# Bidirectional hybrid encoder layer on one core: when the output weights, the convolution's first tile and the first modulation scales are prepared

## The chip, the cores and the metric

One core of a Trainium2 chip runs the whole layer; the other cores are idle. The metric is the time of one execution in microseconds (us), the median of several runs. Engines are called by the profile's names: PE (TensorE), DVE (VectorE), ACT (ScalarE), POOL (GpSimd) and SP (SyncE, which issues all transfers here). Each works through its own instructions in a fixed order and waits where an input or a buffer is not ready.

## What is computed

One transformer-like layer over 2048 tokens of width 1024, in float32:

```
mod = silu(c) @ w_ada + b_ada            # shift1, scale1, gate1, shift2, scale2, gate2
u   = adaln(x) * (1 + scale1) + shift1
q, k, v, glu = split(u @ w_in)
attn = rms(attention(rope(rms(q)), rope(rms(k)), v))      # 8 query heads, 2 kv heads of 64
h    = rms(swish(LN(depthwise31(a * sigmoid(g)))) @ w_pw2)  # 512 channels
x   = LN(alpha*x + gate1 * (concat(attn, h) @ w_o))
ffn = (gelu(conv3(up_g)) * conv3(up_v)) @ w_down            # width 2816
x   = LN(alpha*x + gate2 * ffn)
```

Matrix products run on values that are split into a high part in a matmul format (`wh`, `uh`) and the rest (`wl`, `ul`); each product is three matmuls (`mm3`, L117 to L119). ACT makes the high part (`split`, L123), DVE or POOL subtracts it to get the low part (L126).

## The kernel before, in words

The program has three stages.

**Projections (0 to 400 us).** Sixteen tiles of 128 tokens are normalised, transposed, modulated and multiplied by `w_in`. The modulation vectors come first: `ada_first(hf)` multiplies `silu(c)` with half of the first two blocks of `w_ada`, eight rows of 128 per block, mostly on DVE (L261, L263, tile `acc`) and partly on PE (L266); PE sums over the partitions (L270) and DVE moves shift and scale into `mc[hf]` (L274). For tiles 0 to 2 the products with the first four rows of `w_in` (`lo`) are made as soon as `mc[0]` is there, while `ada_first(1)` still runs. `half(s, 0)` modulates tile s: ACT and POOL each take two of four blocks `u` (L318, L320), then ACT makes `uh`, DVE `ul`. `load_w("kv", True, lo)` loads and splits the key and value columns; `later` holds the two splits of the query columns, whose low parts go to DVE and POOL in turn.

**Attention (400 to 1260 us).** There are 16 units of two heads and 512 queries; each runs 16 steps over blocks of 128 keys (`unit_main`): four score matmuls (L576, L577), two exponentials on ACT (L578, tile `pr`), and four matmuls with the values (L587). Row sums of `pr` are added up by POOL in 12 steps (`lp`, L605 and L608) and by DVE in four (`ld`); in the last unit DVE takes 12 and POOL four. `unit_end` first adds `lp` and `ld` on DVE (L527). After each step `step()` advances three kinds of generators, whose order of `yield` thus sets the order of work: the ends of older units, the preparation of the next unit (`unit_prep`: eight transposes into PSUM, q splits on ACT and DVE L169, 32 matmuls L177 whose maxima DVE reduces in L179, then L186 and L188, which give the next unit's scores their offset), and, from unit 1 on, `conv`.

`conv_work` is one generator: 16 tiles of four groups of channels (`front`: POOL makes the band matrices `tz`, L676, ACT gathers `hg`; `mid`: PE transposes `hg` and ACT writes `hT`; 12 matmuls L695, L701 on DVE), then four chunks (layer norm on DVE, swish, `w_pw2`, norm), and last `load_wo`: for each of 16 pieces of `w_o` DVE multiplies by the gate (L630, tile `rw`), ACT makes `woh`, DVE subtracts (L126, tile `wol`), with two yields a piece. Its line in `step()`:

```
if state["unit"] > 0:
    drain(conv, 2 if state["n"] % 6 == 0 else 1)
```

There are 240 steps from unit 1 on, and in 40 of them `conv` advances twice: 280 advances. The generator has 254 yields.

**Output projection, channel mixer.** `out_mm` multiplies the concatenated heads with `woh` and `wol`; PE's order puts the first of these matmuls among the last steps of the last unit. Then come layer norms and the channel mixer as a Strassen-like product (1450 to 2839 us).

The engine orders are drawn up by a scheduler from the program's order, priorities and its own estimate of durations; `tc.issue_after(ins)` adds that what is traced in the block comes behind `ins` on `ins`'s engine, and leaves other engines free. PSUM has eight banks of 128x512 (`bank()`), handed out in rotation: a matmul into a bank waits for the last reader of what lay there.

Of the kernel before, what the change touches and what calls it, by code (L numbers as in the profile page):

```python
# [13 lines left out]
ALU = mybir.AluOpType  # L14
# [19 lines left out]
def layer_kernel(ctx, tc, x, cT, w_ada, b_ada, b_adaT, w_in, qg2, kg2, rope, conv_t, cmask, mmask,  # L34
# [100 lines left out]
    kv = ExitStack()  # L135
# [58 lines left out]
    with ExitStack() as ph:  # L194
# [36 lines left out]
        def load_w(n, stage=False, ks=range(KD), engines=(V,), wait=False):  # L231
            c0, w = chunks[n]
            kk = D // w
            jobs = []
            for i, k in enumerate(ks[::kk]):
                raw = t4k((P, kk, w), stage)
                SY.dma_start(raw, w_in[k * P:(k + kk) * P, c0:c0 + w].rearrange("(k p) c -> p k c", p=P))
                jobs.append((wih[n][:, k:k + kk, :], wil[n][:, k:k + kk, :], raw, None, engines[i % len(engines)]))
                if not wait:
                    split(*jobs.pop())  # L240
            return jobs
# [4 lines left out]
        def ada_first(hf):  # L246
# [24 lines left out]
                             rhs=ones[:, 0:1], start=False, stop=True, skip_group_check=True)  # L271
            mc[hf] = wks.tile([P, 2, 4], F32, name="mc%d" % hf)
            for v in range(2):
                V.tensor_scalar(mc[hf][:, v], pm[:, v * 4:v * 4 + 4], float(v), None, op0=ALU.add)  # L274

        def ada_later():

# [23 lines left out]
        def normed(xt):  # L301
            mu, r = ln_stats(wks, xt, "ln0")
            nm = wks.tile([P, 1], F32, name="ln0_n", bufs=3)
            G.tensor_scalar(nm, mu, r, -1.0, op0=ALU.mult, op1=ALU.mult)
            A.activation(xt, xt, AF.Identity, scale=r, bias=nm)
            return xt
# [96 lines left out]
        lo, hi = range(4), range(4, KD)  # L403
        xs = [normed(load_x(0)), normed(load_x(1))]
        drain(ada_first(0))
        load_w("kv", True, lo)
        xs.append(load_x(2))
        later = load_w("q", True, lo, (V, G), True)
        ada = ada_first(1)
        next(ada)  # L410
        us = {s: u_tiles() for s in range(3)}
# [15 lines left out]
        for n in ("kv", "q"):  # L427
            for s in range(3):
                if (s, n) == (2, "kv"):
                    normed(xs[2])  # L430
                    flip(2)
                    half(2, 0)
                pss[s, n] = proj(us[s], n, None, lo)
                drain(ada, None if (s, n) == (0, "q") else 1)
# [214 lines left out]
    def conv_work():  # L649
# [32 lines left out]
            A.activation(hT[:, :, 1:129], pq.rearrange("p (g b) -> p g b", g=4), AF.Copy)  # L682

        f = front(0)
        mid(*f)
        for g4 in range(16):
            hT, hg, tz = f
            if g4 < 15:
                f = front(g4 + 1)
            yield  # L690
            pc = bank()
            for i in range(4):
                tv = tz[:, i].rearrange("p (d s) c -> p d (s c)", d=3)
                for d in range(3):
                    T.matmul(pc[:, i * P:(i + 1) * P], lhsT=hT[:, i, d:d + P], rhs=tv[:, d, :],  # L695
                             start=d == 0, stop=d == 2)
                if i == 1:
                    yield
            for i in range(4):
                g = g4 * 4 + i  # L700
                V.tensor_tensor(hc[:, :, g * 8:(g + 1) * 8],  # L701
                                pc[:, i * P:(i + 1) * P].rearrange("p (s c) -> p s c", c=8),
                                cb[:, g * 8:(g + 1) * 8].unsqueeze(1).broadcast_to([P, NT, 8]), op=ALU.add)
            yield
            if g4 < 15:
                mid(*f)
# [88 lines left out]
    def step():  # L795
        with tc.issue_after(state["s"]):
            for e in list(ends):
                if next(e, "end") == "end":
                    ends.remove(e)
            if preps:  # L800
                drain(preps[0][0], 2 if state["n"] % 2 == 0 else 1)
            if state["unit"] > 0:
                drain(conv, 2 if state["n"] % 6 == 0 else 1)
        state["n"] += 1

    for i, (p, c) in enumerate(units):
# [612 lines left out]
```

## Time and profile before

| what | us |
|---|---|
| three runs, median (lowest to highest) | 2837.76 (2829.4 to 2839.68) |
| the profiled execution, its own time | 2841.01 |
| span of that execution's trace | 2839.1 |
| PE busy | 2682.2 (94%) |
| DVE busy | 2229.9 (79%) |
| ACT busy | 1296.5 (46%) |
| POOL busy | 1252.0 (44%) |

The span runs from the first to the last instruction; about 2 us of the execution lie around it. Busy shares are averages over stages that have different limits, so the place where PE stands still, and what ended that wait, says more than the share.

### The profile page before, as it was taken

To read this page: it belongs to the slowest core of one execution; us is meant where nothing else is said; L and a number is where in the kernel's file an instruction comes from. 1 tells how busy PE (TensorE), PEld (TensorE's weight loads), DVE (VectorE), ACT (ScalarE), POOL (GpSimd) and SP (SyncE) were. 2 spreads that over 40 slices of the span, in tenths; PEclk is the share of its full clock that TensorE was granted. 3 is DMA by queue.
4 is the path that set the end of the run, shared out by engine and by line. 5 is a ranking of instruction groups with operands and counts; after the bars stand their busy time and mean duration, and the time that the engine had idled before them with its cause. 6 is when DMAs were issued, how large, how long until landed. Compare 5 with 4: busy or idle time off the path is not lost.

```text
span 2839.1 us, 35217 instructions
## 1 busy us (share of the span) xinstructions
PE 2682.2 (94%) x12108; PEld 2019.5 (71%) x12108; DVE 2229.9 (79%) x3188; ACT 1296.5 (46%) x2562; POOL 1252.0 (44%) x914
## 2 busy tenths in 40 slices
PE   7999998999999999899988999998999998999996
PEld 6777865766565665467866888886888886876774
DVE  7454465566868768837679989999999888889988
ACT  4333323445545554434454544554554555443442
POOL 3544436886857657533535223324322002335234
PEclk9999999999999999999999999999999999999998
DMA  8343241010101112126766443455444236445542
GB/s 272 95 137 111 80 99 30 25 30 19 30 19 27 30 34 78 41 51 180 232 206 224 134 137 127 143 148 164 139 130 149 81 111 208 148 129 158 163 133 65
DMA packets 336867, 320.59 MB, mean 113 GB/s; under 512 B 70688, under 2 KB 244128, under 8 KB 336688
## 3 DMA queue, kind: packets, MB, share of 16 engines
q1 hardware_dynamic: 336688, 318.34, 37.4%
q8 instruction: 95, 1.56, 0.2%
q14 instruction: 84, 0.69, 0.1%
HBM read 225.71 MB, written 92.55 MB: 112 GB/s over the span
## 4 chain that ended last, share of the span: by engine, by line
PE 67%; DVE 16%; issue 5%; DMA 4%; POOL 4%; ACT 2%; SPq 0%; DVEq 0%; ACTq 0%; POOLq 0%
PE b L1082 32%; PE b L587 6%; PE b L117 5%; PE b L118 5%; PE b L119 5%; PE b L177 4%; PE b L576 3%; PE b L577 3%; DVE wl L126 3%; PE b L131 2%; PE b L695 2%; POOL lp L608 1%; DVE mm L179 1%; DVE o L126 1%; DVE ac L1097 1%
## 5 line engine op out<-in xcount | busy, mean ns | idle before, releaser
L1082 PE MATMUL b<-o,wh 128*128 128x512 f32 x3696 | 1157.7, 398 | 58.2 <-ACT wh L123 22.8
L1082 PEld LDWEIGHTS b<-o,wh 128*128 128x128 f32 x3696 | 698.4, 190 | 232.0 <-ACT wh L123 31.3
L1082 PE MATMUL b<-o,wl 128*128 128x512 f32 x1848 | 717.4, 396 | 8.4 <-DVE wl L126 8.3
L1082 PEld LDWEIGHTS b<-o,wl 128*128 128x128 f32 x1848 | 350.5, 190 | 93.9 <-DVE wl L126 14.5
L608 POOL TENSOR_TENSOR lp<-lp,pr 128x1024 f32<-128x1024 f32 x152 | 382.4, 2516 | 77.0 <-ACT pr L578 69.0
L578 ACT ACTIVATE pr<-b 128x512 f32<-128x512 f32 x512 | 278.4, 597 | 291.1 <-PE b L577 278.7
L179 DVE TENSOR_REDUCE mm<-b 128x1 f32<-128x512 f32 x512 | 321.6, 682 | 113.8 <-PE b L177 112.2
L123 ACT ACTIVATE wh<-wr 128x512 fp32r<-128x512 f32 (+2 forms) x456 | 249.8, 569 | 322.0 <-PE b L1082 201.5
L126 DVE TENSOR_TENSOR wl<-wr,wh 128x512 fp32r<-128x512 f32 (+2 forms) x456 | 334.5, 745 | 14.8 <-ACT wh L123 14.6
L587 PE MATMUL b<-pr,vt 128*64 128x512 f32 x1024 | 244.7, 608 | 4.9 <-ACT pr L578 4.9
L1179 POOL TENSOR_TENSOR cb<-cb,g 128x512 f32<-128x512 f32 x44 | 87.2, 2001 | 326.4 <-DMA cb<-in_w_down_dram 317.7
L576 PE MATMUL b<-q,K 128*128 128x512 f32 x512 | 218.0, 427 | 9.6 <-DVE mm L179 5.5
L577 PE MATMUL b<-q,K 72*128 72x512 f32 x512 | 205.9, 404 | 3.0 <-DVE q L188 3.0
L177 PE MATMUL b<-K,q 128*128 128x512 f32 x512 | 165.8, 421 | 6.1 <-DVE mm L179 5.2
L587 PEld LDWEIGHTS b<-pr,vt 128*64 128x64 f32 x1024 | 66.5, 138 | 131.5 <-issue 113.4
L126 POOL TENSOR_TENSOR o<-stg,o 128x512 fp32r<-128x512 f32 x53 | 81.6, 1540 | 161.6 <-ACT o L123 146.0
L177 PEld LDWEIGHTS b<-K,q 128*128 128x128 f32 x512 | 92.1, 192 | 71.5 <-issue 34.1
L123 ACT ACTIVATE o<-stg 128x512 fp32r<-128x512 f32 x177 | 106.4, 627 | 79.1 <-DMA stg<-w_d 47.7
L576 PEld LDWEIGHTS b<-q,K 128*128 128x128 f32 x512 | 99.2, 194 | 57.4 <-issue 17.8
L1059 POOL TENSOR_TENSOR wr<-wr,wr 128x384 f32<-128x384 f32 (+1 forms) x32 | 34.3, 1073 | 238.1 <-DVE s L1056 227.1
L577 PEld LDWEIGHTS b<-q,K 72*128 72x128 f32 x512 | 99.4, 194 | 20.9 <-issue 3.4
L1097 DVE TENSOR_TENSOR ac<-b,ac 128x512 f32<-128x512 f32 x128 | 87.0, 680 | 24.0 <-PE b L1082 24.0
(259 smaller groups left out, 4922.6 us busy)
## 6 DMA issues: line engine op xcount, KB each, us to landing
wr<-in_w_up_dram SPq DMA_DIRECT2D x88, 512.0 KB
stg<-w_d SPq DMA_DIRECT2D x133, 256.0 KB
g_d<-y SPq DMA_DIRECT2D x44, 512.0 KB
w_d<-cb SPq DMA_DIRECT2D x77, 256.0 KB
wr<-g_d SPq DMA_DIRECT2D x96, 192.0 KB
ar<-in_w_ada_dram SPq DMA_DIRECT2D x64, 256.0 KB
cb<-in_w_down_dram SPq DMA_DIRECT2D x44, 256.0 KB
x<-in_x_dram SPq DMA_DIRECT2D x32, 256.0 KB
```

The lines of the kernel that those rows point to most:

```text
L117: T.matmul(ps, lhsT=wh, rhs=mh, start=first, stop=False)
L118: T.matmul(ps, lhsT=wh, rhs=ml, start=False, stop=False)
L123: A.activation(hi, src, AF.Copy)
L126: (el or V).tensor_tensor(lo, src, hi.bitcast(F32), op=ALU.subtract)
L177: T.matmul(px, lhsT=q1[:, i * P:(i + 1) * P], rhs=K1[:, g, kc * 512:(kc + 1) * 512], start=True, stop=True)
L179: V.tensor_reduce(mm[:, h * 4 + i, kc:kc + 1], px, axis=AX, op=ALU.max)
L576: T.matmul(ps, lhsT=k1, rhs=m1, start=True, stop=False)
L577: state["s"] = T.matmul(ps, lhsT=k2, rhs=m2[0:72], start=False, stop=True).ins
L578: ex = state["exp"] = A.activation(pr[:, i, :], ps, AF.Exp, scale=0.125).ins
L587: state["pv"] = T.matmul(po[i * 64:(i + 1) * 64, :], lhsT=vt[:, kt, g * 64:(g + 1) * 64], rhs=pr[:, i, :], start=kt == 0, stop=kt == NT - ...
L608: eng.tensor_tensor(acc, acc, pr, op=ALU.add)
L1082: T.matmul(ps, lhsT=a[x][:, k, :], rhs=b[y][k], start=first and k == 0 and (x, y) == (0, 0), stop=k == nk - 1 and x == 1, skip_group_check ...
```

## The change

Four edits. (1) `mc["last"]` names the last DVE instruction that writes modulation scales (L274); the splits of the first key and value weights, and later the normalisation of tile 2, are traced behind it, which puts them after it on DVE. (2) The second of the two query splits of `later` goes to DVE, no longer to POOL. (3) Four yields are added at the start of `conv_work`: two between `front(0)` and `mid`, two between `mid` and the loop. (4) `conv` advances twice in every tenth step, no longer in every sixth: 24 of the 240 steps, 264 advances in all, against 258 yields.

```diff
@@ ada_first
-                V.tensor_scalar(mc[hf][:, v], pm[:, v * 4:v * 4 + 4], float(v), None, op0=ALU.add)
+                mc["last"] = V.tensor_scalar(mc[hf][:, v], pm[:, v * 4:v * 4 + 4], float(v), None, op0=ALU.add).ins
@@ first tiles
         drain(ada_first(0))
-        load_w("kv", True, lo)
+        with tc.issue_after(mc["last"]):
+            load_w("kv", True, lo)
         xs.append(load_x(2))
-        later = load_w("q", True, lo, (V, G), True)
+        later = load_w("q", True, lo, (V,), True)
...
                 if (s, n) == (2, "kv"):
-                    normed(xs[2])
+                    with tc.issue_after(mc["last"]):
+                        normed(xs[2])
@@ conv_work
         f = front(0)
+        yield
+        yield
         mid(*f)
+        yield
+        yield
@@ step
-                drain(conv, 2 if state["n"] % 6 == 0 else 1)
+                drain(conv, 2 if state["n"] % 10 == 0 else 1)
```

DVE and ACT near 25 us, where the first scales are ready (`mc` is the scale tile, `wl_kv` and `wl_q` low parts of weights, `ln_st` statistics of tile 2, `u`, `uh`, `ul` the modulated tile). DVE before:

```order
L263 SCALAR_TENSOR_TENSOR acc<-ada,cs,acc 128x512 x6
L126 TENSOR_TENSOR wl_kv<-stage,wh_kv 128x1024
L98 BN_STATS ln_st<-x 128x6 x2
L274 TENSOR_SCALAR mc_197<-b 128x4 x2
L100 BN_AGGR ln_mv<-ln_st 128x2
```

DVE now:

```order
L263 SCALAR_TENSOR_TENSOR acc<-ada,cs,acc 128x512 x6
L274 TENSOR_SCALAR mc_197<-b 128x4 x2
L126 TENSOR_TENSOR wl_kv<-stage,wh_kv 128x1024
L98 BN_STATS ln_st<-x 128x6 x2
L126 TENSOR_TENSOR wl_q<-stage,wh_q 128x1024
```

ACT before, from the first split on:

```order
L123 ACTIVATE wh_kv<-stage 128x1024
L123 ACTIVATE wh_q<-stage 128x1024
L318 ACTIVATE u<-x,mc_197 128x128 x2
L123 ACTIVATE wh_q<-stage 128x1024
L123 ACTIVATE uh<-u 128x512
```

ACT now:

```order
L123 ACTIVATE wh_kv<-stage 128x1024
L318 ACTIVATE u<-x,mc_197 128x128 x2
L123 ACTIVATE wh_q<-stage 128x1024
L123 ACTIVATE uh<-u 128x512
L123 ACTIVATE wh_q<-stage 128x1024
```

The scales moved ahead of one split and the statistics, and the first `uh` ahead of the second query split. On POOL, where a query split stood between the blocks `u` of tiles 0 and 1, four `u` now stand in a row.

PE at the border of units 0 and 1, near 447 us, from the transposes of unit 2's queries on (`hg`, `tz`, `hT` belong to the convolution's first tile). Before:

```order
L131 MATMUL b<-ident,qd 128x128 x8
L131 MATMUL b<-ident,hg 128x128 x4
L576 MATMUL b<-q_3752,K_93 128x512
L577 MATMUL b<-q_3753,K_3723 128x512
L576 MATMUL b<-q_3761,K_93 128x512
L577 MATMUL b<-q_3762,K_3723 128x512
L177 MATMUL b<-K_93,q_4081 128x512 x2
L695 MATMUL b<-tz,hT 128x128 x6
```

Now, from the two L177 on (ahead of them stand the same `qd` and score rows):

```order
L177 MATMUL b<-K_93,q_4081 128x512 x2
L578 MATMUL b<-q_3752,K_93 128x512
L579 MATMUL b<-q_3753,K_3723 128x512
L578 MATMUL b<-q_3761,K_93 128x512
L579 MATMUL b<-q_3762,K_3723 128x512
L177 MATMUL b<-K_93,q_4081 128x512 x2
L589 MATMUL b<-pr,vt 64x512 x2
```

The tile's matmuls left this place for one some 30 PE instructions further on, and the next scores stand in their place. DVE's order at this border is as before: `lp<-lp,ld` (L527), then the two L169, then the maxima.

DVE in the last unit, from its first `ld` on. Before:

```order
L605 TENSOR_TENSOR ld<-pr 128x1024
L608 TENSOR_TENSOR ld<-ld,pr 128x1024
L538 TENSOR_TENSOR osq<-osq,l_10565 128x512
L608 TENSOR_TENSOR ld<-ld,pr 128x1024 x4
L522 SCALAR_TENSOR_TENSOR o<-o,agc,b 128x512
L608 TENSOR_TENSOR ld<-ld,pr 128x1024 x5
```

Now:

```order
L607 TENSOR_TENSOR ld<-pr 128x1024
L126 TENSOR_TENSOR wol_10515<-rw,woh_10514 128x512
L610 TENSOR_TENSOR ld<-ld,pr 128x1024
L540 TENSOR_TENSOR osq<-osq,l_10532 128x512
L126 TENSOR_TENSOR wol_10515<-rw,woh_10514 128x512
L632 TENSOR_TENSOR rw<-rw,row_g_10010 128x512
L610 TENSOR_TENSOR ld<-ld,pr 128x1024
L126 TENSOR_TENSOR wol_10586<-rw,woh_10585 128x512
L632 TENSOR_TENSOR rw<-rw,row_g_10010 128x512
L610 TENSOR_TENSOR ld<-ld,pr 128x1024
L126 TENSOR_TENSOR wol_10586<-rw,woh_10585 128x512
L610 TENSOR_TENSOR ld<-ld,pr 128x1024 x2
```

The last six of the 32 `rw` and `wol` instructions moved behind the last unit's first `ld`. Between the first `ld` of units 12 and 13 there were 11 of them, between those of units 13 and 14 the other 21; now none lies in the first stretch, 11 in the second, 15 between the first `ld` of unit 14 and of unit 15.

## Rows read from the trace of the kernel before

**Rows 1.** The page, part 1: busy time, share of the span, instructions.

```profile
PE 2682.2 (94%) x12108; PEld 2019.5 (71%) x12108; DVE 2229.9 (79%) x3188; ACT 1296.5 (46%) x2562; POOL 1252.0 (44%) x914
```

**Rows 2.** Stretches: PE, PEld, DVE, ACT, POOL busy (instructions); PEclk, DMA share, GB/s.

```profile
440.00:460.00 20.00, 12.29 (x57) 8.44 (x56) 7.14 (x9) 6.95 (x15) 13.57 (x6) 0.83 0.12 26
...
620.00:640.00 20.00, 16.13 (x75) 9.19 (x74) 16.23 (x22) 10.29 (x21) 16.11 (x12) 1.00 0.21 60
...
880.00:900.00 20.00, 16.85 (x73) 10.36 (x73) 18.55 (x16) 13.38 (x27) 15.51 (x8) 0.91 0.15 40
...
1120.00:1140.00 20.00, 14.03 (x42) 8.34 (x43) 20.00 (x18) 6.73 (x13) 16.22 (x7) 0.72 0.20 62
1140.00:1160.00 20.00, 17.38 (x67) 9.96 (x67) 19.94 (x24) 7.38 (x14) 12.08 (x5) 0.86 0.19 62
1160.00:1180.00 20.00, 14.41 (x51) 6.48 (x51) 16.24 (x24) 11.81 (x22) 0.53 (x1) 0.83 0.18 58
```

**Rows 3.** The chain of waits, 1100 to 1200 us: shares by line.

```profile
by line: DVE mm L179 19.9%; DVE rw L630 18.3%; PE b L587 13.2%; DVE wol L126 12.9%; PE b L177 7.9%; PE b L576 4.3%; PE b L577 4.0%; POOL lp L608 3.2%; issue 2.7%; DMA rw<-in_w_o_dram 2.6%; DVE ld L605 2.1%; ACT pr L578 1.7%; DVE osq L538 1.
```

**Rows 4.** Tiles rw, wol and lp: duration ns min/median/max, first to last start.

```profile
L630 DVE TENSOR_TENSOR rw<-rw,row_g x16: 673/684/2866, 1102.7 to 1177.5; 128x512 f32<-128x512 f32 x16
L126 DVE TENSOR_TENSOR wol<-rw,woh x16: 671/692/2286, 1106.4 to 1179.6; 128x512 fp32r<-128x512 f32 x16
L608 POOL TENSOR_TENSOR lp<-lp,pr x152: 2337/2384/3290, 412.4 to 1240.5; 128x1024 f32<-128x1024 f32 x152
```

**Rows 5.** Timeline, DVE: first ld of units 4, 12, 13, 14, 15: start, us.

```profile
659.35 3.11 DVE L605 TENSOR_TENSOR ld<-pr 128x1024 f32<-128x1024 f32 x1
...
1079.39 1.22 DVE L605 TENSOR_TENSOR ld<-pr 128x1024 f32<-128x1024 f32 x1
...
1130.60 2.77 DVE L605 TENSOR_TENSOR ld<-pr 128x1024 f32<-128x1024 f32 x1
...
1189.75 2.54 DVE L605 TENSOR_TENSOR ld<-pr 128x1024 f32<-128x1024 f32 x1
...
1215.68 1.23 DVE L605 TENSOR_TENSOR ld<-pr 128x1024 f32<-128x1024 f32 x1 [0.98 <-ACT pr L578]
```

**Rows 6.** Timeline, PE, DVE and POOL, 430 to 460 us [idle before, ended by].

```profile
442.10 2.79 PE L587 MATMUL b<-pr,vt 128*64 128x512 f32 x12 [0.61 <-ACT pr L578]
...
456.08 2.90 PE L695 MATMUL b<-tz,hT 128*128 128x128 f32 x12 [6.51 <-DVE q L169]
...
454.00 1.23 DVE L527 TENSOR_TENSOR lp<-lp,ld 128x1024 f32<-128x1024 f32 x1 [7.11 <-POOL lp L608]
...
432.01 3.27 POOL L676 TENSOR_TENSOR tz<-ct,cm 128x384 f32<-128x384 f32 x4 [5.74 <-DMA ct<-in_conv_t_dram]
435.24 18.73 POOL L608 TENSOR_TENSOR lp<-lp,pr 128x1024 f32<-128x1024 f32 x7
```

**Rows 7.** Timeline, PE, DVE, ACT and POOL, 20 to 40 us.

```profile
29.32 0.58 PE L117 MATMUL b<-wh_kv,uh 128*128 128x256 f32 x1 [5.76 <-ACT uh L123]
...
35.34 0.39 PE L117 MATMUL b<-wh_kv,uh 128*128 128x256 f32 x1 [2.67 <-ACT uh L123]
...
23.53 1.23 DVE L126 TENSOR_TENSOR wl_kv<-stage,wh_kv 128x1024 fp32r<-128x1024 f32 x1 [1.89 <-ACT wh_kv L123]
...
26.19 0.21 DVE L274 TENSOR_SCALAR mc<-b 128x4 f32<-128x4 f32 x2
...
25.97 1.06 ACT L123 ACTIVATE wh_q<-stage 128x1024 fp32r<-128x1024 f32 x1 [2.47 <-DMA stage<-in_w_in_dram]
26.93 0.86 ACT L318 ACTIVATE u<-x,mc 128x128 f32<-128x128 f32 x2
...
34.66 0.63 ACT L123 ACTIVATE uh<-u 128x512 fp32r<-128x512 f32 x1 [2.49 <-POOL u L320]
...
26.57 1.91 POOL L320 TENSOR_SCALAR u<-x,mc 128x128 f32<-128x128 f32 x2 [13.72 <-DVE ln_mv L100]
...
30.09 2.82 POOL L126 TENSOR_TENSOR wl_q<-stage,wh_q 128x1024 fp32r<-128x1024 f32 x1
```

## The prediction

> **What bounds the kernel now.** First I read part 1 of the page: PE is busy for 94% of the span [rows 1]. An edit to DVE or ACT work can therefore pay only where PE stands still or runs at its lower clock. The view of stretches says where that is. Most 20 us stretches of the attention show PE full at a granted clock of 1.00; four places do not [rows 2]: 440 to 460 us (12.29 us busy), 620 to 640 (16.13), 880 to 900 (16.85), and, the largest, 1120 to 1180, where PE is busy for 45.8 of 60 us, its clock averages 0.72, 0.86 and 0.83 of the higher level (2.4 GHz, the rest of the time at 1.2), and DVE is full at 20.00 and 19.94 of 20. The reader is to see there that DVE has become the bound. The chain of waits names the work: of 100 us it gives 18.3% to `rw` and 12.9% to `wol` [rows 3], so 31 us hang on the 32 instructions of the output weights' preparation. They are dearer than they need be. Half of the `rw` take 0.68 us or less, the longest 2.87 [rows 4]; the difference, 2.2 us, is nearly one POOL addition `lp` of 2.38 us.
>
> How much this place loses: the first `ld` of successive units gives the length of a unit [rows 5]. Units 4 to 12 need (1079.39 - 659.35) / 8 = 52.5 us each, with the convolution's four chunks in between. A chunk has 48 matmuls of 512 columns at 2.79 / 12 = 0.23 us [rows 6], 11 us, and 48 smaller ones that I estimate at under half of that each, 5 us: 16 us a chunk, 8 us a unit. A unit without them should need 44.5 us. The stretches from unit 12 to 13 and from 13 to 14 took 51.2 and 59.2 us, 21 us more than two such units.
>
> **Output weights, 6% fewer advances.** `conv` now ends some 5 advances before the end, no longer 25. Nothing is added or removed: the same 32 instructions on DVE, their 16 ACT splits and 16 loads move about one unit later. The stretch from unit 13 to 14 now has what the one from 12 to 13 had: 11 of them and four of the convolution's last products. That one lost 51.2 - 44.5 = 6.7 us, and I take the same. The stretch from unit 14 to 15 gets 15 that were not there. Nine stand ahead of the last offsets (L188), for which unit 15's scores wait; at 31 / 32, about 1 us each, that is 9 us, of which DVE's own idle time there may take 3: 6 us late. The other six of the 15, and the last six of the 32, lie behind everything the scores need; the last unit prepares no successor, and DVE has room, so I cost them at nothing. Should that cover be gone, 12 times 1 us appears at the end of the attention. PE's first use of `woh` stays behind them. The gain is 21 - 6.7 - 6 = 8, say **9 us**. Bounds: 21 if all hides; for the other end, the 26 us between the last two `ld` have room for at most ten POOL additions, and if each holds up a DVE instruction for 2.2 us, 22 us are added to the 15 x 0.68 = 10: 32 us less 3, 29 late, with the 6.7 some 36, 15 worse than now.
>
> **Spreading the convolution.** The slower rate also thins DVE's load in units 1 to 13, where 620 to 640 and 880 to 900 together lose 7.0 us of PE [rows 2]. The order shows no mechanism that removes both, and a chunk's layer norm still falls into one unit. I take **3 us**; bounds -7 (as much again) and 7.
>
> **First tile, four yields.** PE stood still for 6.51 us ahead of the tile's matmuls L695, and one could think that these were early [rows 6]. But the wait ended with L169 on DVE, which frees their PSUM bank, and L169 stood behind L527, which had waited 7.11 us for POOL's last `lp`. POOL worked off seven of these in a row (18.73 us), having waited 5.74 us for a transfer of `ct` before. POOL's and DVE's orders at this border have not changed. What now stands where L695 stood are unit 1's scores, which need the same rotation of banks, and two more matmuls for maxima that DVE reduces only after L527. The matmuls move; the wait does not. I take **0**; bounds -3 (a longer wait behind fewer matmuls) and 7 (all of it).
>
> **Start, scales first.** `mc` was written at 26.19, behind a split that ran from 23.53 and statistics that waited for tile 2 [rows 7]. It can now come at 23.5, 2.7 us earlier. Behind it on DVE are `wl_kv` (1.23 us), the statistics and `wl_q`; for `wl_kv` the first product waits, and at 24.9 it is still ahead of `uh`. Tile 0: ACT's `wh_q` still waits for its transfer until 25.97 and stands ahead of `uh`, which comes at about 27.0 to 27.6; the first product starts at 27.7 in place of 29.32, 1.6 us earlier. Tile 1: POOL had `wl_q` of 2.82 us between the tiles; now four `u` of 0.95 us run from 23.6 to 27.4, ACT has `wh_q` until 28.7, `u` until 29.5, `uh` until 30.1: the second product starts at 30.2 in place of 35.34, 5.1 us earlier. From there PE worked without a break for more than 40 us, so this is what counts, provided that the weights behind it arrive. The split that DVE takes over is 1.23 us beside this. SP's queue has the same transfers, four weight loads ahead of tile 3's rows. I take **5 us**; bounds 0 (transfers set the pace) and 7.
>
> That split reads two SBUF tiles while POOL's `u` runs. The Trainium skill ("SBUF — State Buffer", Who interferes with whom) has a DVE instruction with two SBUF inputs and a POOL instruction that reads SBUF exclude each other for the whole of the instruction. By that rule the low parts of weights wait for up to two `u` of 0.95 us, 1.9 us in all, the start brings 3 and the sum 15. The spread of `rw` [rows 4] is what that rule would give; no row shows it at the start.
>
> **Sum.** 9 + 3 + 0 + 5 = 17 us. The profiled execution took 2841.0 us (span 2839.1 and 2 around it), so 2824.0 by its own time; it lies 3.3 us above the median of the three runs, 2837.76, from which the same 17 give 2820.8. I predict **2821 us**. About 0.5%, 14 us, is what a measurement of this kernel can tell from no change, so the borders are 2824 and 2852.
>
> **Rivals.**
> *The stall moves along.* DVE stays full and the loss of 21 us appears 50 us later: 15 instructions meet POOL's additions in the stretch from unit 14 to 15. For it: the total of DVE work is the same, and half a unit has room for ten additions. Against it: in the last unit four `lp` remain in place of 12, and no maxima. The term of 9 becomes 0, the middle nothing, the start 4: about 2834. By the Trainium skill's rule above (same page) the exclusion decides each meeting; the times between `rw` of 0.68 and of 2.87 agree with it.
> *All of it hides.* 21 + 3 + 7 + 5 = 36 us: 2802. For it: DVE has idle time in the last unit. It needs POOL to be done earlier at the first border, for which I see nothing, or the middle to be free of stalls.
> *Slower.* Unit 15's scores wait for L188 behind the nine moved instructions with nearly every one of ten additions in the way: 15 us worse than now by the bound above, and no product is left in the last unit that PE could run meanwhile. If PE's clock falls there as it fell at 1120 (0.72 for 20 us, which is 11 us at the lower level and costs half, 5 us), it is 20 worse; less 5 at the start: 2853. It decides from the point where the nine take over 2.5 us each; today's mean is 1.
> *It does not do what it says.* At the start the transfers may set the pace, so the scale comes earlier and nothing else: 2826. This I count in the main case.
>
> **How the numbers follow.** The main case, 2808 to 2832, has 0.57; its likeliest value is 2821 and two thirds of it lie below 2824. The stall moving along has 0.27 (2828 to 2838), all hidden 0.12 (2797 to 2808), slower 0.04. Faster by over 0.5%: 0.67 x 0.57 + 0.12 = 0.50, with some 0.03 of the second case at its edge: 0.53. Slower by over 0.5%: half of the slower case, 0.02, rounded up to 0.04 for reorderings in the channel mixer, whose instructions keep their work but swap neighbours. Within: 0.43. The range that should hold 8 of 10 is 2804 to 2837: it takes in most of the first two cases and half of the third.
>
> **What would show it.** Right: `mc` at 23.5 to 24, the second product near 30; the wait of some 6 us near 450 still there with L169 or the maxima as its end; 1120 to 1140 with PE near full; `rw` and `wol` from about 1140 to 1225, and a loss of 10 to 15 us between 1140 and 1200. Wrong: a wait for DVE inside the last unit, a gap ahead of the first `woh` matmul, a second product that waits for a transfer, or a change of over 5 us after 1450 us.

## The result, and the profile after

The changed kernel takes **2849.63 us** (median of 6 runs, 2847.25 to 2852.32), the kernel before 2833.76 on the same chip (6 runs, 2829.4 to 2839.68). The ratio is 1.0055, 95% interval 1.004 to 1.007: slower by just over half a percent, outside the predicted range. The profiled execution took 2852.3 us (span 2850.5), that of before 2841.0. Line numbers from 404 on are 1 higher than before, from 431 on 2, in the convolution 6: L632 is L630, L610 is L608, L733 is L727.

The page, part 1, hardly differs from that of before [rows 1]. What changed is where PE stands still and where its clock falls:

```profile
PE 2692.2 (94%) x12108; PEld 2021.9 (71%) x12108; DVE 2229.0 (78%) x3189; ACT 1296.9 (45%) x2562; POOL 1252.6 (44%) x913
```

The view of stretches of the changed kernel (columns as in [rows 2]):

```profile
60.00:80.00 20.00, 17.70 (x76) 14.54 (x77) 14.75 (x31) 10.81 (x17) 12.37 (x17) 0.83 0.67 187
80.00:100.00 20.00, 15.16 (x61) 12.07 (x60) 15.19 (x25) 8.75 (x18) 17.41 (x22) 0.83 0.40 126
...
680.00:700.00 20.00, 17.33 (x64) 9.13 (x65) 10.90 (x17) 9.73 (x18) 15.52 (x8) 0.83 0.16 41
...
760.00:780.00 20.00, 16.63 (x62) 10.90 (x61) 15.53 (x21) 6.79 (x13) 10.26 (x6) 0.74 0.05 13
...
1120.00:1140.00 20.00, 19.24 (x89) 11.67 (x88) 12.68 (x21) 10.09 (x19) 10.51 (x3) 1.00 0.00 1
1140.00:1160.00 20.00, 20.00 (x98) 11.85 (x98) 15.65 (x25) 9.85 (x19) 19.39 (x8) 1.00 0.31 85
1160.00:1180.00 20.00, 17.12 (x68) 9.15 (x66) 16.46 (x19) 12.35 (x22) 9.80 (x5) 0.91 0.37 113
1180.00:1200.00 20.00, 16.47 (x62) 9.85 (x58) 19.51 (x18) 7.18 (x15) 16.94 (x7) 0.83 0.24 78
1200.00:1220.00 20.00, 14.79 (x54) 7.59 (x54) 20.00 (x23) 7.98 (x14) 12.98 (x6) 0.91 0.12 41
```

The full DVE and the empty PE of 1120 to 1160 [rows 2] are gone, and stand again at 1180 to 1220. New are 60 to 100 us and 680 to 700, both at a clock of 0.83, and at 760 to 780 more is lost than before, with the clock down to 0.74. The same stretches of the kernel before:

```profile
60.00:80.00 20.00, 20.00 (x102) 16.75 (x102) 14.66 (x29) 10.59 (x18) 13.64 (x15) 1.00 0.66 199
80.00:100.00 20.00, 17.69 (x79) 13.99 (x78) 13.65 (x26) 6.18 (x13) 12.48 (x19) 1.00 0.57 151
...
760.00:780.00 20.00, 17.74 (x77) 10.82 (x77) 19.10 (x25) 11.62 (x21) 16.26 (x9) 0.91 0.04 14
```

The timeline of PE gives the waits behind them in the changed kernel (in brackets the idle time and what ended it):

```profile
62.28 0.58 PE L117 MATMUL b<-wh_kv,uh 128*128 128x256 f32 x1 [4.11 <-ACT uh L123]
...
90.24 0.80 PE L117 MATMUL b<-wh_g,uh 128*128 128x512 f32 x1 [4.84 <-DVE qn L352]
...
464.80 0.80 PE L578 MATMUL b<-q,K 128*128 128x512 f32 x1 [5.60 <-DVE q L169]
...
764.58 0.79 PE L177 MATMUL b<-K,q 128*128 128x512 f32 x1 [3.37 <-DVE mm L179]
...
1188.03 1.84 PE L545 MATMUL b<-blk,osq 128*128 128x2 f32 x8 [3.22 <-DVE osq L540]
...
1221.82 0.70 PE L186 MATMUL b<-ident,mz 128*72 128x128 f32 x2 [3.58 <-DVE mz L182]
```

**A yardstick for every run.** From the starts of PE's matmuls in each trace I add up matmul work (0.2325 us per matmul of 512 columns, 0.118 of 256, 0.135 of 128) and ask how much later than in the first profile of before a kernel starts the matmul that follows the same amount of work. The table gives this lag, in us (minus: ahead), at places named by the time of before. A place whose number grows lost time. Work moved in the order shifts single values by some us for a while (at 1170 the output weights' stall lies ahead in one kernel, behind in the other); the last column is the span less 2839.1.

| profile | 36 | 57 | 95 | 342 | 423 | 680 | 859 | 1069 | 1170 | 1249 | end |
|---|---|---|---|---|---|---|---|---|---|---|---|
| changed | -3.0 | -2.7 | 9.0 | 9.0 | 10.6 | 10.6 | 19.0 | 18.1 | -4.1 | 18.9 | 11.4 |
| x1 start | -3.2 | -3.4 | 9.4 | 9.4 | 11.0 | 13.8 | 10.8 | 10.4 | 9.2 | 7.9 | 4.4 |
| x2 scales | -0.7 | -2.7 | 5.0 | 5.0 | 7.8 | 5.3 | 2.3 | 2.3 | 3.2 | 2.8 | 3.7 |
| x3 rate | -0.2 | 0.1 | -0.8 | -0.8 | 2.0 | -2.4 | 2.8 | 3.1 | -6.9 | 6.5 | 11.3 |
| x4 yields | 0.2 | 0.9 | 3.6 | 3.7 | 6.6 | 0.5 | 6.1 | 12.8 | 10.0 | 14.8 | 13.2 |
| x5 before again | 0.8 | -3.6 | 1.3 | 1.3 | 2.9 | 1.5 | -1.5 | -1.7 | -3.5 | -4.8 | -6.8 |
| x6 hold | -2.7 | -3.0 | 1.9 | 2.0 | 2.1 | -0.4 | 8.6 | 7.3 | -15.0 | 7.7 | -3.6 |
| x7 query on POOL | -0.1 | -2.1 | 5.1 | 5.1 | 6.5 | 6.2 | 16.2 | 14.9 | -7.3 | 14.8 | 7.1 |
| x8 sparse | -0.7 | -0.2 | -1.0 | -0.9 | 1.9 | 0.2 | 3.2 | 9.9 | 13.6 | 11.5 | 10.7 |
| x9 changed, few lp | -3.5 | -2.1 | 10.4 | 10.5 | 12.0 | 4.0 | 0.6 | -7.3 | -30.6 | -22.3 | -33.8 |
| x10 before, few lp | 1.7 | 1.3 | 2.9 | 3.0 | 5.8 | 2.1 | -2.5 | -10.0 | -23.2 | -24.7 | -26.1 |
| x11 dense | 0.4 | 1.6 | 2.2 | 2.2 | 2.3 | 3.1 | 3.4 | 11.8 | -10.2 | 12.6 | 11.3 |
| x12 scales, qa buffers | -0.7 | -2.7 | 3.0 | 3.0 | 4.7 | 2.9 | -0.1 | -0.3 | -1.0 | -1.3 | -5.6 |
| x13 hold, qa buffers | -3.2 | -2.0 | 0.8 | 0.8 | 2.5 | 4.7 | 1.7 | 3.6 | 3.1 | 1.7 | -4.5 |
| x14 before, qa buffers | -1.4 | -5.5 | 0.7 | 0.7 | 3.5 | 0.8 | -2.2 | -2.2 | -2.1 | -2.0 | -11.2 |

Each row is one profile, so chance has to be known. Many of these kernels have, in a part, the same instructions in the same order on PE, DVE, ACT and POOL, so what lies between their profiles there is chance (or what an earlier part hands on):

- Up to 400 us before, x3, x4, x5, x8, x10 and x11 are alike, with lags of -0.9 to 3.7 at 342. So are the changed kernel, x1 and x9 (9.0 to 10.5), and x2 and x7 (5.0 and 5.1).
- In the middle, 423 to 1069, before, x1, x2 and x5 are alike (their lag changes by 0 to -5.5), and the changed kernel, x6 and x7 (7.5, 5.2 and 8.4 lost).
- In the channel mixer, 1249 to the end, there are four orders: before, x1, x5, x10 (0 to 3.5 won); changed, x4, x12, x13, x14 (1.6 to 9.2 won); x2, x3, x7, x8, x11 (4.8 lost to 7.7 won); x6, x9 (11.3 and 11.5 won).

So one profile differs from the next by up to about 5 us in the start and the middle, and by up to 12 in the mixer, with nothing changed there.

The changed kernel lost 9.0 at the start, 1.6 from 342 to 423 (as x5 did), 7.5 in the middle and 0.8 from there to the end of the attention, and won 7.5 in the channel mixer. Against x5, the second profile of the kernel before, it lost 12.1 in the middle and 3.9 at the output weights.

### The profile page after: what moved, and what is told of

The parts are those of the page before. It is cut to its first block, busy times and chain, and to the rows that moved or that the text cites. A ratio compares the mean times of both kernels' runs of the same rounds, so it can differ in the third digit from the quotient of the medians.

```text
span 2850.5 us, 35197 instructions
## 1 busy us (share of the span) xinstructions
PE 2692.2 (94%) x12108; PEld 2021.9 (71%) x12108; DVE 2229.0 (78%) x3189; ACT 1296.9 (45%) x2562; POOL 1252.6 (44%) x913
## 4 chain that ended last, share of the span: by engine, by line
PE 50%; DVE 17%; issue 4%; DMA 3%; POOL 2%; ACT 2%; SPq 0%; DVEq 0%; ACTq 0%; POOLq 0%
PE b L1088 29%; PE b L589 5%; DVE wl L126 3%; PE b L578 3%; PE b L177 3%; PE b L579 3%; PE b L117 2%; PE b L118 2%; PE b L119 2%; DVE mm L179 1%; DVE o L126 1%; DVE y L1147 1%; PE b L131 1%; DVE ac L1103 1%; DMA stg<-w_d 1%
## 5 line engine op out<-in xcount | busy, mean ns | idle before, releaser
L1088 PE MATMUL b<-o,wh 128*128 128x512 f32 x3696 | 1151.4, 396 | 51.3 <-ACT wh L123 22.8
L1088 PE MATMUL b<-o,wl 128*128 128x512 f32 x1848 | 714.9, 395 | 14.1 <-DVE wl L126 13.8
L610 POOL TENSOR_TENSOR lp<-lp,pr 128x1024 f32<-128x1024 f32 x152 | 386.2, 2541 | 79.2 <-ACT pr L580 71.7
L126 DVE TENSOR_TENSOR wl<-wr,wh 128x512 fp32r<-128x512 f32 (+2 forms) x456 | 336.7, 748 | 11.9 <-ACT wh L123 11.4
L177 PE MATMUL b<-K,q 128*128 128x512 f32 x512 | 164.0, 421 | 6.7 <-DVE mm L179 3.9
L177 PEld LDWEIGHTS b<-K,q 128*128 128x128 f32 x512 | 93.7, 194 | 68.0 <-issue 27.6
L126 DVE TENSOR_TENSOR o<-stg,o 128x512 fp32r<-128x512 f32 x124 | 106.3, 879 | 2.3 <-ACT o L123 2.3
```

Of the source, the lines that this page charges most:

```text
L126: (el or V).tensor_tensor(lo, src, hi.bitcast(F32), op=ALU.subtract)
L177: T.matmul(px, lhsT=q1[:, i * P:(i + 1) * P], rhs=K1[:, g, kc * 512:(kc + 1) * 512], start=True, stop=True)
L610: eng.tensor_tensor(acc, acc, pr, op=ALU.add)
L1088: T.matmul(ps, lhsT=a[x][:, k, :], rhs=b[y][k], start=first and k == 0 and (x, y) == (0, 0), stop=k == nk - 1 and x == 1, skip_group_check ...
```

## The experiments

### The four edits, one group at a time (x1 to x4), and before again (x5)

x1 is before with edits 1 and 2 of the diff, x2 with edit 1, x3 with the tenth step alone, x4 with the four yields alone; x5 is the kernel before, unchanged.

> Before with edits 1 and 2 alone (scales ahead, both query low parts on DVE). Theory S: the loss of the start is ACT's order. With both edits two wh_g splits stand ahead of the second half's first u, and wh_g or wh_a ahead of each uh, and these splits wait for weight transfers, so PE runs dry near 58 and 85 us and its clock falls: PE 9 us behind the kernel before from 100 us to the end of the projections, as in the changed kernel; total 2843 (9 above 2834). Rival: the loss at the start comes from the convolution's edits (memory or priorities): PE level or 3 ahead at 100 us, 2830 to 2834.

> Before with edit 1 alone; the second query split stays on POOL. Theory S: ACT's order has no g split ahead of the second half's u here, so no wait near 58 us; PE 2 to 6 us ahead of before at 100 us, total 2828 to 2832. Rival: the earlier start itself outruns the weights (the transfers set the pace, and what is won is given back as a wait and a lower clock): PE 4 to 9 us behind at 100 us, total 2838 to 2843.

> Before with the rate alone (every tenth step advances twice). Theory M: the chunks of the convolution fall on other steps of the units, and the stalls for DVE's maxima near 680 and 765 us of the changed kernel come from there: nothing at the start, some 6 to 10 us lost between 600 and 900 us, the output weights' stall moved to 1160 to 1240 with its size kept (20 us): total 2838 to 2846. Rival (my prediction's terms): 9 + 3 gained, 2822.

> Before with the four yields alone, the rate left at every sixth step. Theory: the border near 450 us keeps its wait of 5.6 to 6.5 us; later everything comes four advances, a quarter of a unit, later. If the middle's loss comes from where chunks fall on the units, this shift too may cost or bring some 5 us there: 2829 to 2841. Rival: the yields are what costs the middle its 10 us: 2842 to 2846.

> The kernel before once more, unchanged, to see how far one profile of it differs from another in each part. If the offsets of the other runs are effects of their orders, PE's place in its own work differs by under 1 us at 300 us and by under 3 us at 1250 us from the first profile; if they are chance, by 5 to 10 us.

| run | us | before, same chip | ratio, 95% interval |
|---|---|---|---|
| x1 | 2844.04 | 2836.98 | 1.0023, 1.0014 to 1.0032 |
| x2 | 2847.11 | 2836.98 | 1.0038, 1.0025 to 1.0052 |
| x3 | 2850.91 | 2836.98 | 1.0048, 1.0033 to 1.0063 |
| x4 | 2847.54 | 2836.98 | 1.0035, 1.0023 to 1.0048 |
| x5 | 2834.23 (one run) | 2838.11 | |

Every part alone is slower than before, by 7 to 14 us, and they do not add up: the whole is 16 slower.

**Start.** x1 repeats the changed kernel's 9 us there, far outside the -0.9 to 3.7 of the seven kernels with the old order, so these belong to edits 1 and 2. x1's orders differ from those of before between 24 and 106 us alone, and its median is 7.1 above. The timeline of ACT in the changed kernel shows the first half of them:

```profile
51.22 1.06 ACT L123 ACTIVATE wh_g<-stage 128x1024 fp32r<-128x1024 f32 x1 [1.18 <-DMA stage<-in_w_in_dram]
...
52.95 1.04 ACT L123 ACTIVATE wh_g<-stage 128x1024 fp32r<-128x1024 f32 x1
53.90 0.61 ACT L123 ACTIVATE uh<-u 128x512 fp32r<-128x512 f32 x1
56.65 1.06 ACT L123 ACTIVATE wh_g<-stage 128x1024 fp32r<-128x1024 f32 x1 [2.13 <-DMA stage<-in_w_in_dram]
57.62 0.86 ACT L318 ACTIVATE u<-x,mc 128x128 f32<-128x128 f32 x2
60.66 1.06 ACT L123 ACTIVATE wh_a<-stage 128x1024 fp32r<-128x1024 f32 x1 [2.18 <-DMA stage<-in_w_in_dram]
61.62 0.61 ACT L123 ACTIVATE uh<-u 128x512 fp32r<-128x512 f32 x1
```

The tile's second half `u` is made at 57.62, but its `uh` stands behind a split of `wh_a` that waits for a transfer until 60.66. PE gets `uh` 4.11 us too late. Five splits of `wh_g` and `wh_a` stand ahead of this `uh`; in the order of before only two did. The order of x2 has them in the old way too, and there the wait near 58 us is absent, as expected; but x2 loses its lead at one place further on, where the expected 2 to 6 us ahead became 5.0 behind (x7, with the same order, 5.1). PE of x2:

```profile
87.13 0.80 PE L117 MATMUL b<-wh_g,uh 128*128 128x512 f32 x1 [8.45 <-DVE qn L352]
```

**Middle.** Between 423 and 1069 x3 loses 1.1 and x4 6.2, the three kernels with both edits (changed, x6, x7) 5.2 to 8.4, while the kernels with the old order (before, x1, x2, x5) stand between 0 and -5.5. So the middle's loss belongs to edits 3 and 4. The yields alone are outside what chance gave, though in one profile, that of the slowest of x4's six runs; the rate alone is hardly outside. x4 is also 3.7 behind at 342, but up to 440 us its orders are those of before: this is chance.

### ACT's splits held back (x6), the query split back on POOL (x7)

x6 adds to the changed kernel (the name `mark` holds the last `uh` that ACT makes for the second half):

```diff
-        load_w("g", True)
-        load_w("a", True, range(KD), (V, V, G, V))
+        with tc.issue_after(mark[0]):
+            load_w("g", True)
+            load_w("a", True, range(KD), (V, V, G, V))
```

x7 has `(V, G)` in place of `(V,)` for the query columns again.

> The changed kernel, in which ACT's splits of the g and a weights are put behind the second half's last uh. Theory S (ACT's order): the wait of 4.1 us near 58 us is gone and PE is still 2 to 3 us ahead of before at 65 us. The wait near 85 us is another one (query products that hold the PSUM banks until qn): it stays or grows, so that at 100 us PE is 2 to 6 us behind before in place of 9; total 2843 to 2847. Rival (the weights' transfers set the pace): the wait near 58 us stays or becomes one for wh_q or wh_g, 9 behind at 100 us, total 2850.

> The changed kernel with edit 2 undone: the second query split back on POOL. ACT's order at the start is then that of the run with edit 1 alone. Theory S: no wait near 58 us, 4 to 6 us behind before at 100 us in place of 9, the rest of the attention as in the changed kernel: total 2843 to 2847. Rival (the start's loss comes from edit 1 alone): 9 behind, 2850.

x6 takes 2839.81 us to 2838.11 of before (1.0001, 0.9986 to 1.0015): the 16 us are gone. Its lag at 342 is 2.0 in place of 9.0, so ACT's order is shown to be the cause of seven of the nine. Of the other 8.0 us between the two profiles, 3.8 lie in the channel mixer and 2.3 in the middle, no more than chance gives there. The next wait is not `qn`, as I had expected, but one for the last weights, which now come later; PE of x6:

```profile
79.98 0.79 PE L118 MATMUL b<-wl_a,uh 128*128 128x512 f32 x1 [3.95 <-POOL wl_a L128]
```

x7 has the start of x2, 5.1 behind at 342 as expected; its total of 2852.10 (1.0061, 1.0041 to 1.008) is above what I expected, with 8.4 lost in the middle.

### The output weights spread (x8) or drawn together (x11)

x8 has two more yields for each piece of `w_o` and every fifth step double. x11:

```diff
                 V.tensor_tensor(raw, raw, g1[:, sl], op=ALU.mult)
-                yield
                 split(woh[k][:, sl], wol[k][:, sl], raw)
                 yield
...
-                drain(conv, 2 if state["n"] % 6 == 0 else 1)
+                drain(conv, 2 if state["n"] % 24 == 0 else 1)
```

> The kernel before, with four yields in place of two for each piece of the output weights, and two advances in every fifth step (288 for 286 yields). Theory W: the loss at the output weights is DVE's load in one unit (21 instructions beside maxima and additions); spread over 3.3 units in place of 1.7 they cost under 8 us in place of 21 there, and the middle may lose up to 10 by another alignment: total 2822 to 2838. Rival: each of the 32 costs what it meets (POOL's addition), however they are spread: the 21 us stay, 2837 to 2847.

> The kernel before with one yield in place of two for each piece of the output weights and two advances in every 24th step (250 for 238 yields): the 32 instructions come later and closer together, more of them in the last unit, which has no maxima and four additions of POOL. If what costs them is the maxima and POOL's additions of a normal unit, the loss of 21 us falls by 8 to 15, and the convolution is thinner: 2820 to 2834. If PE then waits for the first woh, or the first 20 still meet ten additions in half a unit: 2838 to 2850.

x8 is slower, 2854.98 (1.0056, 1.0037 to 1.0075), but decides nothing: the view of tile `rw` shows the instructions from 1101 to 1179 us as in [rows 4], so they were not spread at all.

```profile
L630 DVE TENSOR_TENSOR rw<-rw,row_g x16: 675/682/2884, 1101.1 to 1178.9; 128x512 f32<-128x512 f32 x16
```

x11, 2852.95 (1.0057, 1.004 to 1.0074), moved them, and is the changed kernel once more: it wins 22.0 us from 1069 to 1170 and gives 22.8 back until 1249 (the changed kernel 22.2 and 23.0). A stretch of it and its tile:

```profile
1200.00:1220.00 20.00, 13.54 (x51) 7.47 (x50) 16.51 (x16) 9.19 (x18) 11.05 (x4) 0.83 0.17 58
```

```profile
L630 DVE TENSOR_TENSOR rw<-rw,row_g x16: 673/684/2827, 1175.3 to 1245.0; 128x512 f32<-128x512 f32 x16
```

Twice the instructions moved later, and twice the stall moved with them at its size. In x11 19.5 us are lost ahead of the last unit (from 1187 to 1217 in before's time) and 5.2 in it.

### POOL's additions left out (x9, x10)

In both kernels, from unit 1 on, POOL makes only the first of a unit's additions `lp` (26 of the 168 are left, eleven of them in unit 0); the row sums therefore lack the other blocks.

```diff
+            elif key == "g" and first[key] is None and state["unit"] > 0:
+                pass
             elif first[key] is not None:
```

> The changed kernel, in which POOL adds up only the first two blocks of each unit's row sums from unit 1 on (11 of 12 or more additions lp a unit are left out, so the sums are not those of the reference). Theory L: the stalls at the chunks' layer norms (near 765 us) and at the output weights (1170 to 1225) come from POOL's additions holding up DVE: rw, wol and the layer norms' hc (up to 3 us today) fall to 0.7 us each, and the end of the attention comes 25 to 40 us earlier than in the changed kernel. Rival D: DVE's own load in those units (21 added instructions, maxima) is enough: the long instructions go, but more than half of the loss at the output weights (12 us or more) stays.

> The kernel before with the same additions of POOL left out. Theory L: its stalls near 630, 770, 890 us and at 1120 to 1180 shrink too, and what then lies between this and the changed kernel without additions is the start alone: 6 to 12 us at the end of the attention, 0 to 3 us of it from the middle and the output weights. Rival D: the two differ by 15 or more, since where the instructions stand in the units decides.

One run each: x9 2807.10 us, x10 2815.12, before 2838.83. Without these additions the changed kernel is **8 us faster** than the kernel before under the same treatment; with them it is 16 slower. The runs of one kernel differ by up to 17 us, so two single runs show that the 16 are gone, but not that 8 are won. Nor do the 8 come from the additions alone: x9 is 7.5 behind x10 at the start and wins 10.1 more in the channel mixer. What bears on the additions is 342 to 1249, where x9 gains 5.1 us more than x10 (32.8 against 27.7) and the changed kernel lost 9.9 against before. What DVE pays is seen in the layer norms' tile `hc`, first of the changed kernel, then of x9:

```profile
L733 DVE TENSOR_SCALAR hc<-hc,cl_mv,cl_r x16: 510/608/2687, 643.8 to 1024.1; 128x512 f32<-128x512 f32 x16
```

```profile
L735 DVE TENSOR_SCALAR hc<-hc,cl_mv,cl_r x16: 512/535/2160, 644.0 to 995.7; 128x512 f32<-128x512 f32 x16
```

All 16 together take 19.6 us in the changed kernel, 17.2 in before, 10.2 in x9 and 9.2 in x10; the 32 `rw` and `wol` take 39.0, 38.7, 29.6 and 26.5. They did not all fall to 0.7 as I had expected, and the timelines of DVE and POOL in x9 say why:

```profile
1140.98 2.88 DVE L126 TENSOR_TENSOR wol<-rw,woh 128x512 fp32r<-128x512 f32 x1
...
1150.97 2.86 DVE L634 TENSOR_TENSOR rw<-rw,row_g 128x512 f32<-128x512 f32 x1
...
1154.53 2.08 DVE L126 TENSOR_TENSOR wol<-rw,woh 128x512 fp32r<-128x512 f32 x1
```

```profile
1140.85 2.46 POOL L126 TENSOR_TENSOR ml<-mr,mh 128x1024 fp32r<-128x1024 f32 x1 [25.48 <-ACT mh L123]
1150.53 2.76 POOL L126 TENSOR_TENSOR ml<-mr,mh 128x1024 fp32r<-128x1024 f32 x1 [7.21 <-ACT mh L123]
1153.26 2.81 POOL L609 TENSOR_TENSOR lp<-pr 128x1024 f32<-128x1024 f32 x1
```

Each long one on DVE begins while one of the three long POOL instructions that are left here runs, and ends about 0.55 us behind it. In the changed kernel it is the same: of the 48 `hc`, `rw` and `wol`, the 17 that take over 1 us all meet a POOL instruction of 128x1024, and the 25 that meet none are short. Not one of the 512 maxima, which read PSUM, is ever longer than 0.70 us there, though 228 of them begin while such a POOL instruction runs:

```profile
L179 DVE TENSOR_REDUCE mm<-b x512: 650/681/696, 377.7 to 1216.1; 128x1 f32<-128x512 f32 x171
```

The Trainium skill ("SBUF — State Buffer", Who interferes with whom) lists this: two SBUF inputs meet POOL, a tensor_scalar can, a tensor_reduce does not. The rows above agree, with 2.69 us in place of 0.51 for a tensor_scalar.

Theory L holds for `hc`, `rw` and `wol`, which lose their long times where no POOL instruction is left to meet. Rival D does not hold: from 1069 to 1249 x9 wins 15.0 us and x10 14.7 against before, so some 6 of the prediction's 21 stay, and at 1249 the two are 2.4 apart, not 15. At 1140 to 1160 of x9, where the three long ones lie, DVE is still full and PE is busy for only 15.88 us, the largest gap left. One thing x9 and x10 do not separate: DVE's waits for the sums themselves (idle time that ended with POOL's `lp`, from 480 us on) also went, 6.4 us in the changed kernel and 9.4 in before, none in x9 and x10.

```profile
1140.00:1160.00 20.00, 15.88 (x64) 8.45 (x63) 19.90 (x23) 10.41 (x18) 8.00 (x3) 0.97 0.34 106
```

### The queries' squares in buffers of their own (x12 to x14)

In x2 ACT makes the squares `qa` of the first two tiles at 65 and at 81 us, the second only after DVE's rotation `qr` of the first has read the one buffer. The timeline of ACT:

```profile
81.31 0.60 ACT L345 ACTIVATE qa<-b 128x512 f32<-128x512 f32 x1 [5.88 <-DVE qr L389]
```

Until `qn` is made, the query product keeps its PSUM bank. x12 (x2), x13 (x1 with the hold of x6) and x14 (before) let the squares use the three buffers of `qr`:

```diff
-            sq = wk.tile([P, n, 64], F32, name=tag + "a", bufs=nb)
+            if tag == "q":
+                sq = wk.tile([P, n, 64], F32, name="qa", tag="qr", bufs=3)
+            else:
+                sq = wk.tile([P, n, 64], F32, name=tag + "a", bufs=nb)
```

> Before with edit 1 alone, and the squares of the queries (qa) in the three buffers of qr instead of the one that the rotation qb also uses. Theory Q (the chain through one buffer holds PSUM banks): tile 1's qa follows its product at once, the wait of 8.45 us for qn at 87 us falls below 2, and PE is 2 to 4 us ahead of before at 100 us instead of 4.6 behind; total 2828 to 2836, 6 or more below the run with edit 1 alone in its distance to before. Rival (load of POOL and DVE in this stretch): the wait stays at 5 us or more, total as with edit 1 alone, 10 above before.

> Before with edits 1 and 2, ACT's g and a splits held behind the second half's last uh, and the buffers of the run above. Theory Q with theory S: neither wait of the start is left, PE is 2 to 4 us ahead of before at 100 us; total 2828 to 2836, the convolution's order being nearly that of before. Rival: a later transfer or the norms' load takes the lead back: level with before, 2836 to 2842.

> The kernel before with these buffers alone. Its own wait near 82 us is 1.8 us, for kn and not for qn: theory Q gives 0 to 2 us at 100 us, total 2834 to 2842, so that what the two runs above gain over this is the start edits' own share. Rival: the buffers themselves bring 5 us or more whatever the start, 2830 or less.

| run | us | before, same chip | ratio, 95% interval |
|---|---|---|---|
| x12 | 2840.01 | 2838.57 | 1.0004, 0.9991 to 1.0018 |
| x13 | 2836.62 | 2838.57 | 0.9987, 0.9977 to 0.9997 |
| x14 | 2833.97 | 2838.57 | 0.9987, 0.9976 to 0.9998 |

The wait for `qn` in x12 is half of what it was:

```profile
84.14 0.79 PE L117 MATMUL b<-wh_g,uh 128*128 128x512 f32 x1 [4.53 <-DVE qn L355]
```

So theory Q is half right, the chain is one part of that wait. In x13 it is gone, and a wait of 2.90 us for `wl_a` stands there. Each kernel with edit 1 is 2.0 to 3.4 us ahead at 57 us and none is ahead at 95: the lead of the start is always taken back by one of three things, `uh` behind the splits (changed, x1, x9), the queries' norm (x2, x7, x12), or the last weights (x6, x13). That is x13's rival. Even without edit 1 it goes so: x5 and x14 were 3.6 and 5.5 ahead at 57 and are 1.3 and 0.7 behind at 95. x14 is 0.13% below before, and x13 as far. In x14's profile, which lies 4.3 us below its median, 9.2 us are won in the channel mixer, where its order is that of the changed kernel, x4, x12 and x13 (1.6 to 7.5 won); so where its gain comes from is not settled.

## Why the prediction was wrong

**Start, predicted 5 won, measured 9 lost.** The first step was right: `mc` came at 23.4 us, and PE was 3.0 ahead at 36. The sentence that failed is "From there PE worked without a break for more than 40 us, so this is what counts, provided that the weights behind it arrive". Earlier matmuls are worth something only if the next thing that PE waits for is early too. I read ACT's order to the fifth split; the `uh` that decides is the sixteenth. x6 gives seven of the nine back by that order alone, x12 and x13 show what is behind it. In each wait PE's clock also fell: it averages 0.83 over 20 us in both stretches, where before showed 1.00 and 1.00. That is 6.8 us at the lower level each time, some 3 of them lost.

**First tile, 0, measured 0.** The matmuls L695 moved, the wait stayed: 5.60 us at 464.80 for L169, in front of the scores, where it was 6.51 [rows 6] (x6, with the same order, has 6.8). This point was right in place and cause.

**Middle, 3 won, measured 7.5 lost (12.1 against x5).** "The slower rate also thins DVE's load" failed. The waits at 625, 632 and 889 us (two of the losses of [rows 2]) and one at 773 became others at 683, 765 and 808 us, fewer and two of them longer. The stretches 423 to 1069 of before and the same work in the changed kernel:

```profile
423.00:1069.00 646.00, 623.26 (x3073) 401.95 (x3072) 451.75 (x693) 315.49 (x590) 457.81 (x271) 0.99 0.11 28
```

```profile
433.60:1087.10 653.50, 630.13 (x3051) 399.68 (x3051) 446.84 (x699) 316.10 (x592) 468.90 (x273) 0.98 0.11 27
```

PE stands still for 22.7 us in the one and for 23.4 in the other, so the 7.5 us are not idle time. The granted clock is at its lower level for 13.7 us of the first and for 30.7 of the second (the 0.99 and 0.98 of the rows). At the lower level a matmul of `pr` and `vt` starts 0.41 us after the last, in place of 0.23, one of `q` and `K` 0.48 in place of 0.26; so 17 us more there lose 7 to 8 us of work. x7, with the same order, repeats it (24.8 us idle, 30.7 at the lower level), x6 in part (26.2 and 20.5). My prediction counted PE's idle time in the middle and left out its clock: that term was missing. One of the places is 760 to 780, with 0.74. At 756.62 three `hc` of a layer norm, made ready at the border of two units, meet POOL's first additions of the new unit, and take 7.30 us in place of 1.5; maxima wait behind them, and PE for these. DVE and POOL in the changed kernel:

```profile
756.62 7.30 DVE L733 TENSOR_SCALAR hc<-hc,cl_mv,cl_r 128x512 f32<-128x512 f32 x3
763.85 1.27 DVE L179 TENSOR_REDUCE mm<-b 128x1 f32<-128x512 f32 x2
```

```profile
756.14 2.36 POOL L607 TENSOR_TENSOR lp<-pr 128x1024 f32<-128x1024 f32 x1 [0.76 <-PE b L537]
758.58 2.45 POOL L610 TENSOR_TENSOR lp<-lp,pr 128x1024 f32<-128x1024 f32 x1
761.30 2.34 POOL L610 TENSOR_TENSOR lp<-lp,pr 128x1024 f32<-128x1024 f32 x1 [0.28 <-ACT pr L580]
```

I had put both ends of this term at 7. Mean load says nothing about such a meeting; what counts is which DVE instructions stand at the border where POOL works without a gap. Meetings of `hc` are not the whole cause: in x4 the 16 `hc` take only 13.6 us, and its middle lost 6.2. In x9 and x10, without the additions, PE stands still for 11.5 and 11.4 us there and is at the lower clock for 6.8 in each, and x9's middle is better than x10's by 3.5 (19.3 won against 15.8). That fits additions that hold up DVE; which of their effects costs the rest stays open.

**Output weights, 9 won, measured 0.8 lost (3.9 against x5).** The step that failed is the 6 us for the stretch from unit 14 to 15: nine instructions at "about 1 us each", of which "DVE's own idle time there may take 3". Between the first `ld` of unit 14 (1194.16) and the last offsets the nine took 17.4 us, six of them 1.7 to 2.9, and DVE had no idle time at all. DVE (the long ones) and POOL there:

```profile
1195.30 2.87 DVE L126 TENSOR_TENSOR wol<-rw,woh 128x512 fp32r<-128x512 f32 x1
1198.09 2.86 DVE L632 TENSOR_TENSOR rw<-rw,row_g 128x512 f32<-128x512 f32 x1
...
1206.10 2.87 DVE L632 TENSOR_TENSOR rw<-rw,row_g 128x512 f32<-128x512 f32 x1
...
1218.84 2.83 DVE L126 TENSOR_TENSOR wol<-rw,woh 128x512 fp32r<-128x512 f32 x1
```

```profile
1191.77 16.65 POOL L610 TENSOR_TENSOR lp<-lp,pr 128x1024 f32<-128x1024 f32 x6
1215.13 5.99 POOL L610 TENSOR_TENSOR lp<-lp,pr 128x1024 f32<-128x1024 f32 x2 [6.70 <-ACT pr L580]
```

PE's lag grows from 4.9 us at 1194 to 18.4 at 1229. That the other twelve "lie behind everything the scores need" was right: from there to the end of the attention the lag grows by 0.5. The rival *the stall moves along* is what happened; the 32 instructions cost 39.0 us, where before took 38.7.

```profile
L632 DVE TENSOR_TENSOR rw<-rw,row_g x16: 677/692/2870, 1163.0 to 1244.6; 128x512 f32<-128x512 f32 x16
L126 DVE TENSOR_TENSOR wol<-rw,woh x16: 675/682/2865, 1168.5 to 1246.3; 128x512 fp32r<-128x512 f32 x16
```

PE's waits at 1188 and 1221 end with DVE. The gain was there until 1170 (22.2 us), and 23.0 went back by 1249; x6 and x7, with the same order, show 22.3 and 22.7, 22.2 and 22.1. The first `ld` was a poor yardstick: DVE's order places it freely, and in unit 12 it lay 8.5 us later than before, while PE lay 18 later.

**Channel mixer, 0, measured 7.5 won.** The prediction has instructions there that "keep their work but swap neighbours", at nothing. Kernels with one and the same order there differ as much: from 4.8 lost (x3) to 7.7 won (x7). So the 7.5 are not shown to come from the change. They go with the clock: it is at its lower level for 68.6 us of this part in before, 52.0 in the changed kernel, 86.7 in x3 and 49.2 in x14, while PE's idle time is 74.0, 71.3, 72.2 and 71.7. Why the clock falls more often in one execution than in another stays open.

**The range** left out the case that the start loses: I gave that term 0 to 7, so my slower case had to come from the last unit alone and got 0.04. The sum of measured terms, -9.0 - 1.6 (342 to 423) - 7.5 - 0.8 + 7.5 = -11.4, is the difference of the two spans; the other 4.5 of the 15.9 between the medians come from the two profiled executions: that of before lies 7.2 above its median, that of the changed kernel 2.7.

## What to carry to other kernels

Follow an instruction that is made earlier to the next wait of the engine it feeds, in the new order and past the piece that was edited; a lead that meets a later gate is worth nothing, and can cost the clock. Price work that is moved on DVE by what POOL runs at the new place, not by its mean, and expect a stall that DVE's load and POOL's additions make together to move with it. Count what a wait does to the clock, not only how long it lasts. Where a scheduler draws up the whole order, an edit in one stage changes the order of others (x4's four yields, in the attention, changed that of the mixer), and even an unchanged order takes another time from run to run: give each untouched stage a range too (here some 10 us for the mixer), of both signs, and compare the orders of two kernels before a difference is put down to them.

## What the runs showed of the hardware that I had not expected

A DVE instruction with one tensor input, the layer norms' `hc`, is held up by POOL's additions as those with two are: 0.51 to 2.69 us. PE's clock can cost more than the waits beside it: the middle lost 7.5 us with 0.7 us more of idle time and 17 us more at the lower level. And POOL's row sums cost this kernel much more than POOL's own time suggests: with most of them left out, the kernel before ends 24 us earlier (one run, 2815.12 against 2838.83), though POOL is busy for only 44% of the span [rows 1] and those of the changed kernel's PE waits that are shown above end with DVE or ACT.
